# A hybrid RWKV-7 / gated-DeltaNet / SwiGLU layer on one core: the order of high and low products, the width of a small inversion step, the place of the scans' output products, and the planner's estimates

## The chip, the core and the metric

The kernel runs on one core of a Trainium2 chip. The metric is the time of one execution in microseconds (us). Three runs of the kernel before gave 2196.24 us in the median (2191.26 to 2198.05). One execution was recorded by the hardware profiler.

The engines are named as the profile names them: PE does matrix products (PEld is its loading of the stationary operand, which overlaps), DVE is the vector engine, ACT the scalar engine, POOL does a few fills and copies, and SP issues nearly all DMAs.

## What is computed

One layer of a backbone over 256 latent tokens and 256 context tokens, model width 2048. All inputs and outputs are fp32. Cut to what matters:

```python
h  = modulate(rmsnorm(x, norm1_w), sh1, sc1);  hc = the same for ctx
rw, cv, z, ab, gt = split(h @ w_in)              # and of hc @ w_in
# branch a: RWKV-7, 16 heads of 64, forward and backward scans, context before latent
s = s * w_t - (s @ kk_t) b_t + v_t k_t;   y_t = s @ r_t
# branch b: gated DeltaNet, 8 heads of 128, chunks of 64, forward and backward
u, wk = triangular_solve(I + strict(kb k^T * decay), [v * beta, kb * exp(g)])
v_new = u - wk @ s;  o = q_dec @ s + qk @ v_new;  s = s * g_last + k_tail^T @ v_new
m = sigmoid(g_a) * (o_a @ p_a) + sigmoid(g_b) * (o_b @ p_b)
x = x + gt1 * (m @ w_out)
x = x + gt2 * swiglu(modulate(rmsnorm(x, norm2_w), sh2, sc2), w_gate_up, w_down)
return rmsnorm(x, final_norm_w)
```

## The kernel before

**Two-part products.** Every product with a large weight matrix is done with operands split in two: a value is cast to fp32r (the high part, `whi` for weights and `hxh`, `hch` for activations), and what the cast left over is the low part (`wlo`, `hxl`, `hcl`). A product is then high*high + weight-high*activation-low + weight-low*activation-high, three matmuls of 128x128x256 for each 128 rows of depth. For a weight tile ACT casts `whi` from the loaded `wraw`, and after it DVE subtracts to get `wlo`; both work on quarters of four depth blocks (128x512).

**Stages.** (1) Norms, modulation and the first narrow products (0 to about 124 us of the span). (2) One long stage, "the weave" (lines 329 to 1830, from 124.5 to 1337.5 us), with the input projection, both token mixers, and the merge products. (3) The rest of the merge, the output projection and the feed-forward part, in an order written out by hand (1337.5 us to the end at 2188.6).

**The weave and its planner.** Each piece of work of stage 2 is a Python generator that yields operations (`Op`), lists of them, pauses, or things it waits for (a PSUM bank, a named event). `Weave.run` (line 274) is a list scheduler that runs when the program is built: it keeps a clock for each engine, picks the piece whose next operation could start first by its own estimates (`Lane.product`, `Lane.cost` and the table `LAT`), breaks ties by rank, and emits it. What it emits is the order of the instructions on PE, DVE, ACT and POOL; the chip keeps that order and waits on semaphores. So the estimates set an order and never a time. The line number of almost every instruction of the weave is that of the helper which emits it (L164), so groups are told apart by their tiles.

**The pieces that matter here.**
- `products` (line 1255) runs the large products in a stream: `k`, `v`, `r` for eight pairs of RWKV heads, `K`, `V`, `Q` for eight DeltaNet heads, `g` for gates, and later `p`, `b`, `f`, `l` for the merge. For each quarter it waits until the cast of `whi` and `wlo` has been emitted, then for each depth block it issues high*high, high*low and low*high in turn. `cast` (line 1164) fills `whi` and `wlo`, of which there are four quarters each (rings `his`, `los`); both are handed back at the quarter's end.
- `invert` (line 635) inverts unit triangular 64x64 blocks, 16 of two halves for a pair of RWKV heads (`inverse`), 8 for a DeltaNet head (`head_inverse`). Blocks of 16 are inverted on DVE, then merged 16 to 32 and 32 to 64 by small PE products. The 16-to-32 step takes the list `fours` (line 694): one 32x32 stationary part with 16 moving columns for each unit, half and block; a first run of them, two SCALAR_TENSOR_TENSOR on DVE (`Qm`), and a second run. For a pair of heads a run has 64 matmuls, for a DeltaNet head 32.
- `scan` (line 1017) walks the chunks of two pairs of heads at once, in nine calls of four steps. A step has a first group of PE products (`VX` by `LAl` or `LAc`), a copy on ACT to `R1`, products of that with the inverse (`Tx`), then a group with an identity and with the scan's outputs (stationary `VX`, moving `LAl`), copies to `VX` on ACT, and a third group whose sums DVE scales into the next `VX` and adds into the output `Y`. The sums live in PSUM banks `psb` (two): the first is taken at the step's start, the second (`acc`) after the products with the inverse.

Matmuls whose stationary part is smaller than 128x128 use a part of the array; going from one such part size to another, or to the full array and back, is called a turn below.

Of the kernel before, what the change touches and what calls it, by code (L numbers as in the profile page):

```python
# [18 lines left out]
P = 128  # L19
# [11 lines left out]
LAT = dict(dma=3.1, v=1.0, s=1.0, hop=dict(e=0.215, v=0.135, s=0.15, g=0.1), slack=0.1, own=0.09, grp=32, crank=-1, cg=4, into=0.14, back=0.2, cross=0.14, stay=0.0, gpace=1.6)  # L31
# [74 lines left out]
class Op:  # L106


    def __init__(self, lane, cost, call, mode=None, base=None):
        self.lane, self.cost, self.call, self.mode, self.base = lane, cost, call, mode, base  # L110


class Lane:
# [5 lines left out]
    def product(self, out, a):  # L119
# [8 lines left out]
        if rows < 64:  # L128
            return 0.0165, mode
        if rows == 64:  # L130
            return (0.064 if n > 64 else 0.048) if m < P else 0.02 + n * 4 / 2400, mode
        return (0.06 if m < 64 else 0.058), mode
# [17 lines left out]
    def __getattr__(self, name):  # L150

        def op(out, *a, **k):
# [4 lines left out]
            mode = base = None  # L157
            if name == "transpose" and len(a) == 2:
                cost, mode = 0.109, "full"
            elif name == "matmul":  # L160
                cost, mode = self.product(out, a)
            else:
                cost, base = self.cost(name, out, a, k), (out.offset // out.ap[0][0], out.shape[0])
            return Op(self, cost, lambda: getattr(self.engine, name)(out, *a, **k), mode, base)  # L164
# [53 lines left out]
class Weave:  # L218


    def __init__(self):
        self.work, self.free, self.done, self.now, self.mode, self.cur, self.idle = [], {}, {}, 0.0, "full", None, True
# [45 lines left out]
    def release(self, banks):  # L268
        banks.free.append(self.cur.shown())

# [3 lines left out]
    def run(self):  # L274
        while self.work:
# [37 lines left out]
            for o in ops:  # L313
                if lane is self.tensor:
                    cost += self.turn(o.mode)
                    self.mode = o.mode
# [12 lines left out]
def emit(ctx: ExitStack, tc, A, out, dbg=None):  # L329
# [305 lines left out]
    def invert(pool, Lt, parts, nu, which, full, fill, half_way=None, early=None):  # L635
# [53 lines left out]
        def Nt_(h, u):  # L689
# [4 lines left out]
        fours = [(h, u, 32 * b, slice(64 * h + 32 * b, 64 * h + 32 * b + 32)) for u in range(nu) for h in range(2) for b in range(2)]  # L694
        qm = pool.tile([P, 256], F32, tag="qm", name="Qm") if half_way else xt
        Qm = qm[:, :16 * nu].rearrange("p (u c) -> p u c", c=16)
        ps = yield pib
        pv = ps[:, 0:32 * nu].rearrange("p (k u c) -> p k u c", k=2, c=16)
        yield [e.matmul(pv[r, 0, u], Lt(h, u)[b:b + 32, b:b + 32], T0[r, u, b + 16 * (u // h2):b + 16 * (u // h2) + 16],
                        start=True, stop=True) for h, u, b, r in fours]  # L700
        for d in range(2):
            yield v.scalar_tensor_tensor(Qm[:, us[d]], pv[:, 0, us[d]], low16[:, d:d + 1],
                                         eye16[:, d].unsqueeze(1).to_broadcast([P, h2, 16]), ALU.mult, ALU.add)
        yield [e.matmul(pv[r, 1, u], Tx[r, u, b:b + 32], Qm[r, u, :], start=True, stop=True) for h, u, b, r in fours]
        for h in range(2):
            yield [(s.copy if h else v.tensor_copy)(T0[r, us[d], b + 16 * d:b + 16 * d + 16], pv[r, 1, us[d]])
                   for d in range(2) for b in (0, 32) for r in (slice(64 * h + b, 64 * h + b + 32),)]
# [21 lines left out]
        qo = qm[:, 128:256].rearrange("p (i c) -> p i c", c=32) if half_way else pool.tile([P, h2, 32], F32, tag="ivo", name="qo")  # L729
# [75 lines left out]

    def lowrank_out(p, j, ps, so):
# [4 lines left out]
        if j == 3:  # L811
            weave.ready("lowrank", p)
# [204 lines left out]
    def scan(r):  # L1017
# [25 lines left out]
        for m in range(4):  # L1043
# [5 lines left out]
            ops = []  # L1049
            for q, o, n, vx, la, cs_ in todo:  # L1050
                for d, j, h in dh:
                    w = slice(0, P) if n else half[1 - j]
                    ops.append(e.matmul(ps[h, P * q + 64 * d:P * q + 64 * d + 64], la[d][w, cm[d], j, 0:64],
                                        vx[w, 4 * d + cm[d], j, :], start=True, stop=True))
            yield ops
            R1 = rs.tile([P, T], F32, tag="y2", name="R1")
            yield s.copy(R1[:, part], ps[:, part])
            yield [e.matmul(ps[h, T + P * q + 64 * d:T + P * q + 64 * d + 64], o["Tt"](j, 8 * d + cs_[d]),
                            R1[h, P * q + 64 * d:P * q + 64 * d + 64], start=True, stop=True)
                   for q, o, n, vx, la, cs_ in todo for d, j, h in dh]  # L1060

# [8 lines left out]
            for q, o, n, vx, la, cs_ in todo:  # L1070
                if 0 < n < 7:
                    for j, h in enumerate(half):
                        ops.append(add(c3(acc[h, P * q:P * q + P]), j, ident[h, h], vx[h, both, j, :]))
# [4 lines left out]
            if ops:  # L1078
                yield ops
# [66 lines left out]
    gate_next = iter(range(40))  # L1146

    def gate_out(pool, j, ps):
# [4 lines left out]
        if j == 39:  # L1153
# [10 lines left out]
    def cast(parts, i):  # L1164

        for q, part in enumerate(parts):
# [5 lines left out]
            yield s.copy(hi[:, :n], raw[:, :n])  # L1172
            lo = yield los
            yield v.tensor_sub(lo[:, :n], raw[:, :n], hi[:, :n].bitcast(F32))
            raws.put(raw)
            casts[i, q] = hi, lo
            weave.ready("cast", i, q)
# [77 lines left out]
    def products():  # L1255
# [53 lines left out]
        while todo or ahead:  # L1309
# [8 lines left out]
            if what == "l":  # L1318
                yield "cast", i, 0
                hi, lo = casts.pop((i, 0))  # L1320
# [771 lines left out]
```

## Time and profile before

| | |
|---|---|
| median of three runs | 2196.24 us |
| profiled execution, first to last instruction (span) | 2188.6 us |
| median less span | 7.6 us |
| stage 1 / the weave / stage 3 | 124.5 / 1213 / 851 us |
| DVE, ACT busy over the span | 71%, 51% |
| PE instructions in the profile | 24536 matmuls, 24536 weight loads |

The page gives no time of its own for the profiled execution apart from its span. An fp32 matmul shows as two records in the profile, an fp32r matmul as one. The view of groups lists instructions by line, engine and tiles, with the busy time, the mean length and the idle time just before them; the view of waits lists who waited for whom; the timeline lists instructions in order of time; the view of windows gives each engine's busy time and the granted PE clock in a stretch. PE's ends are modelled and overlap the next start, so the distance from start to start is what one matmul costs.

### The profile page before, as it was taken

What the parts mean: (1) busy time and instruction counts of PE and PEld (TensorE: products, weight loads), DVE (VectorE), ACT (ScalarE), POOL (GpSimd) and SP (SyncE); (2) the same over time, 40 slices, a digit from 0 to 9 for tenths busy, and PEclk for the clock granted to TensorE, in tenths of its full rate; (3) what the DMA queues carried; (4) which work ended last, traced back from release to release, by engine and by line L of the source; (5) the groups of instructions that cost most, each with busy time, mean ns of one, the idle gap of its engine ahead of it and who ended that gap; (6) DMA issues with size and microseconds to landing.
All of it is one profiled execution on the core that took longest, in us unless ns stands there. A gap on an engine that the chain in (4) does not pass through costs nothing.

```text
span 2188.6 us, 59116 instructions
## 1 busy us (share of the span) xinstructions
PE 2108.6 (96%) x24536; PEld 1977.7 (90%) x24536; DVE 1552.5 (71%) x3308; ACT 1118.2 (51%) x2209; POOL 19.2 (1%) x55
## 2 busy tenths in 40 slices
PE   7999999999999999999999998999999999999997
PEld 5897698889888888998989987999999999999997
DVE  4466589889889976899998776865666665555554
ACT  3246654565455556565565754644444444444443
POOL 0000000000000000000000000000000000000000
PEclk9999999999999999999999999999999999999999
DMA  9966756645555554665653754856777776666665
GB/s 377 415 175 196 228 154 179 178 144 156 154 167 143 166 164 135 188 194 171 176 152 112 216 153 157 297 177 201 238 248 235 242 241 217 194 191 194 195 194 163
DMA packets 276286, 431.14 MB, mean 197 GB/s; under 512 B 119857, under 2 KB 136625, under 8 KB 271665
## 3 DMA queue, kind: packets, MB, share of 16 engines
q1 hardware_dynamic: 262192, 402.19, 59.5%
q10 hardware_dynamic: 13824, 25.17, 3.6%
q8 instruction: 192, 3.15, 0.6%
q14 instruction: 78, 0.63, 0.1%
HBM read 401.50 MB, written 25.77 MB: 195 GB/s over the span
## 4 chain that ended last, share of the span: by engine, by line
PE 80%; DVE 7%; DMA 7%; ACT 3%; issue 2%; SPq 0%; DVEq 0%; ACTq 0%
PE mm L164 26%; PE mm L438 12%; PE mm L436 12%; PE mm L437 12%; PE s L164 6%; PE pa L164 5%; PE pi L164 3%; DVE arena L164 2%; DMA wraw<-w 2%; DVE wlo L164 2%; DMA wraw<-ada_rest 1%; PE mm L529 1%; PE s L579 1%; ACT arena L164 1%; PE mm L579 1%
## 5 line engine op out<-in xcount | busy, mean ns | idle before, releaser
L427 DVE TENSOR_TENSOR wlo<-wraw,whi 128x1024 fp32r<-128x1024 f32 (+1 forms) x264 | 314.9, 1193 | 291.0 <-ACT whi L426 291.0
L426 ACT CAST whi<-wraw 128x1024 fp32r<-128x1024 f32 (+1 forms) x264 | 270.6, 1025 | 386.1 <-PE mm L437 359.5
L164 PE MATMUL mm<-hxh,wlo 128*128 128x256 f32 x1376 | 399.9, 291 | 9.5 <-DVE wlo L164 7.7
L164 PE MATMUL mm<-hxh,whi 128*128 128x256 f32 x1376 | 397.0, 288 | 2.3 <-ACT whi L164 1.3
L164 PE MATMUL mm<-hxl,whi 128*128 128x256 f32 x1376 | 395.4, 287 | 0.0
L438 PE MATMUL mm<-hfh,wlo 128*128 128x256 f32 x1344 | 371.8, 277 | 0.2 <-DVE wlo L427 0.2
L436 PE MATMUL mm<-hfh,whi 128*128 128x256 f32 x1344 | 371.2, 276 | 0.0
L437 PE MATMUL mm<-hfl,whi 128*128 128x256 f32 x1344 | 371.2, 276 | 0.0
L164 ACT CAST whi<-wraw 128x512 fp32r<-128x512 f32 (+1 forms) x398 | 242.8, 616 | 214.9 <-PE mm L164 93.2
L164 DVE TENSOR_TENSOR wlo<-wraw,whi 128x512 fp32r<-128x512 f32 (+1 forms) x398 | 270.3, 682 | 86.2 <-ACT whi L164 79.8
L164 PEld LDWEIGHTS mm<-hxh,wlo 128*128 128x128 f32 x1376 | 260.7, 189 | 19.6 <-DVE wlo L164 11.3
L164 PEld LDWEIGHTS mm<-hxh,whi 128*128 128x128 f32 x1376 | 260.6, 189 | 10.3 <-issue 4.3
L164 PEld LDWEIGHTS mm<-hxl,whi 128*128 128x128 f32 x1376 | 260.8, 190 | 6.3 <-issue 3.9
L438 PEld LDWEIGHTS mm<-hfh,wlo 128*128 128x128 f32 x1344 | 252.4, 188 | 1.2 <-DVE wlo L427 0.8
L437 PEld LDWEIGHTS mm<-hfl,whi 128*128 128x128 f32 x1344 | 252.5, 188 | 0.0
L436 PEld LDWEIGHTS mm<-hfh,whi 128*128 128x128 f32 x1344 | 252.4, 188 | 0.0
L164 PE MATMUL mm<-hch,wlo 128*128 128x256 f32 x496 | 142.5, 287 | 0.0
L164 PE MATMUL mm<-hcl,whi 128*128 128x256 f32 x496 | 142.2, 287 | 0.0
L436 PE MATMUL mm<-za,whi 128*128 128x256 f32 x512 | 141.5, 276 | 0.0
L164 PE MATMUL mm<-hch,whi 128*128 128x256 f32 x496 | 141.3, 285 | 0.2 <-issue 0.2
L438 PE MATMUL mm<-za,wlo 128*128 128x256 f32 x512 | 141.3, 276 | 0.0
L437 PE MATMUL mm<-za,whi 128*128 128x256 f32 x512 | 141.3, 276 | 0.0
(407 smaller groups left out, 4534.2 us busy)
## 6 DMA issues: line engine op xcount, KB each, us to landing
wraw<-w SPq DMA_DIRECT2D x344, 256.0 KB, 3.3
wraw<-wgu SPq DMA_DIRECT2D x168, 512.0 KB, 4.7
aw<-ada_first SPq DMA_DIRECT2D x32, 1024.0 KB, 12.2
wraw<-wdn SPq DMA_DIRECT2D x64, 448.0 KB, 3.7
wraw<-ada_rest SPq DMA_DIRECT2D x96, 256.0 KB, 3.2
aw<-ada_rest SPq DMA_DIRECT2D x48, 512.0 KB, 4.4
wraw<-wout SPq DMA_DIRECT2D x64, 256.0 KB, 5.7
aw<-ada_gt ACTq DMA_DIRECT2D x64, 256.0 KB, 5.0
```

Of the source, the lines that this page charges most:

```text
L164: return Op(self, cost, lambda: getattr(self.engine, name)(out, *a, **k), mode, base)
L426: S.copy(hi[:, c, :M], raw[:, c, :M])
L427: V.tensor_sub(lo[:, c, :M], raw[:, c, :M], hi[:, c, :M].bitcast(F32))
L436: E.matmul(ps, hi, Xh[:, k, :n], start=first and i == 0, stop=False)
L437: E.matmul(ps, hi, Xl[:, k, :n], start=False, stop=False)
L438: E.matmul(ps, lo, Xh[:, k, :n], start=False, stop=last and i == len(wt) - 1)
L529: E.matmul(ps[32 * g:32 * g + 32, 0:P], ckr[:, k].rearrange("p a b -> p (a b)"), aws[e, c][:, i, g], start=k == 0, stop=k == KT - 1)
L579: E.matmul(ps[:m, T * a:T * a + T], w_, X[:, 2 * e + k, :], start=e == k == i == 0, stop=e == NE - 1 and k == 1 and i == len(todo) - 1)
```

## The change

Four things are changed in the weave; stages 1 and 3 are as before.

**1. High first, low last.** In a quarter all products with `whi` are issued first and those with `wlo` after them. The piece waits for the cast of `whi` at the quarter's start and for that of `wlo` between, and hands each ring back on its own.

Below is PE's order in the merge products `mm<-oa` (the activation's high and low part share the tile `oa_...`, with tile numbers to tell quarters apart). Before:

```order
L164 MATMUL mm_17143<-oa_16582,whi_1610 128x256 x2
L164 MATMUL mm_17143<-oa_16582,wlo_1612 128x256
L164 MATMUL mm_17143<-oa_16582,whi_1611 128x256 x2
L164 MATMUL pa_17165<-arena_1603,CR_81 128x256
L164 MATMUL mm_17143<-oa_16582,wlo_1613 128x256
L164 MATMUL mm_17143<-oa_16582,whi_1611 128x256
```

and of the change:

```order
L170 MATMUL mm_16420<-oa_15756,wlo_1613 128x256 x4
L170 MATMUL mm_16420<-oa_15756,whi_1611 128x256
L170 MATMUL s_16440<-St_16412,arena_1603 128x128 x2
L170 MATMUL mm_16420<-oa_15756,whi_1611 128x256 x7
L170 MATMUL mm_16420<-oa_15756,wlo_1613 128x256 x4
```

The first `wlo` product of a quarter stood behind two products of that quarter; it stands behind eight now (behind sixteen where latent and context tokens go together, as in `k`, `v`, `K`, `V`; behind four there before).

**2. The 16-to-32 step on 64x64 parts.** One matmul with a 64x64 stationary part and 32 moving columns takes the place of two with 32x32 and 16.

PE's order at the first run of this step, in the inversion of the second pair of heads (`pi` is the PSUM bank). Before:

```order
L164 MATMUL mm<-hxh,wlo 128x256
L164 MATMUL mm<-hxh,whi 128x256
L164 MATMUL mm<-hxl,whi 128x256
L164 MATMUL pi<-arena 32x16 x64
L164 MATMUL mm<-hxh,wlo 128x256
L164 MATMUL pa<-C,arena 128x128 x2
```

and of the change:

```order
L170 MATMUL mm<-hxh,wlo 128x256 x2
L170 MATMUL pa<-LAl,arena 64x128 x16
L170 MATMUL mm<-hxh,wlo 128x256 x2
L170 MATMUL mm<-hxh,whi 128x256
L170 MATMUL mm<-hxl,whi 128x256
L170 MATMUL pi<-arena 64x32 x32
```

The run has half as many matmuls. Over the whole program there are 19443 matmuls before and 18675 now, 768 fewer, all of them here: 16 runs that go from 64 to 32 and 16 that go from 32 to 16.

**3. The scans' outputs in the first group.** A step takes both PSUM banks at its start, issues the output products behind `VX` by `LAl`/`LAc`, and issues the identity's products in one list with those by the inverse.

PE's order in one step of a scan. Before:

```order
L164 MATMUL s<-VX,LAl 64x64 x4
L164 MATMUL s<-VX,LAc 64x64 x4
L164 MATMUL mm<-hxh,whi 128x256
L164 MATMUL mm<-hxl,whi 128x256
L164 MATMUL pa<-LAl,arena 64x128 x16
L164 MATMUL s<-R_7194,Tx 64x64 x8
L164 MATMUL s<-VX,C 64x128 x4
L164 MATMUL s<-LAl,VX 64x64 x4
L164 MATMUL mm<-hxh,wlo 128x256
```

and of the change:

```order
L170 MATMUL s<-VX,LAl 64x64 x4
L170 MATMUL s<-VX,LAc 64x64 x4
L170 MATMUL s<-LAl,VX 64x64 x4
L170 MATMUL pa<-C,arena 128x128 x2
L170 MATMUL pa<-wraw,CR 32x256 x2
L170 MATMUL mm<-hxh,wlo 128x256
L170 MATMUL s<-R_6016,Tx 64x64 x8
L170 MATMUL s<-VX,C 64x128 x4
L170 MATMUL pa<-C,wraw 128x64 x2
```

The outputs (`s<-LAl,VX`, 128 stationary rows by 64) moved from behind the 64x64 parts to the group that has their own part size. In the weave's order a turn from one small part size to another occurs 87 times before and 51 times now; visits of small parts from the full array are 230 and 237.

**4. Estimates and order.** `LAT` has other costs of turns, `product` other costs of small parts, a new function `fetched` makes the planner's PE wait for 256-instruction pieces of its program, and `Weave.add` shifts each piece's rank by a drawn number of up to 8 (`NUDGE`). Two events (`lowrank`, `gates`) count their parts instead of naming the last one.

The diff, cut to its core:

```diff
-LAT = dict(dma=3.1, ..., into=0.14, back=0.2, cross=0.14, stay=0.0, gpace=1.6)
+LAT = dict(dma=3.1, ..., into=0.1, back=0.22, cross=0.115, stay=0.0, gpace=1.6, fetch=3.6, land=2.3)
+NUDGE = (46, 8.0)
...
     def add(self, rank, gen, at=None):
         now, cur = self.now, self.cur
+        if cur is None and rank < 800:
+            rank += NUDGE[1] * (2 * self.draw.random() - 1)
...
+    def fetched(self, t, n):
+
+        self.inst += n
+        while self.inst > 256 * self.chunk + 200:
+            self.asked = max(t, self.asked + LAT["fetch"])
+            self.lands.append(self.asked + LAT["land"])
+            self.chunk += 1
+        return max(t, self.lands[(self.inst - 1) // 256])
...
-        fours = [(h, u, 32 * b, slice(...)) for u in range(nu) for h in range(2) for b in range(2)]
+        units = [(h, u, half[h]) for u in range(nu) for h in range(2)]
...
-        yield [e.matmul(pv[r, 1, u], Tx[r, u, b:b + 32], Qm[r, u, :], start=True, stop=True) for h, u, b, r in fours]
+        yield [e.matmul(second[r, 32 * u:32 * u + 32], Tx[r, u], Qm[r, 32 * u:32 * u + 32], start=True, stop=True) for h, u, r in units]
...
             ps = yield psb
+            acc = yield psb
...
+            for q, o, n, vx, la, cs_ in todo:
+                if n >= 4:
+                    for d, j, h in dh:
+                        ops.append(add(acc[h, T + 64 * d:T + 64 * d + 64], j, vx[:, 4 * d + cm[d], j, :], la[d][:, cm[d], j, 64:P]))
             yield ops
...
-            acc = yield psb
...
-            for k in range(nk):
-                if k % CG == 0:
-                    ask(NQ, k == nk - CG)
-                    yield "cast", i, k // CG
-                    hi, lo = casts.pop((i, k // CG))
-                for j, (w, part) in enumerate(((hi, 0), (hi, 1), (lo, 0))):
...
+            for q in range(0, nk, CG):
+                ask(NQ, q == nk - CG)
+                for t, ring, parts in (("h", his, (0, 1)), ("l", los, (0,))):
+                    yield t, i, q // CG
+                    w = casts.pop((t, i, q // CG))
+                    for k in range(q, q + CG):
+                        for part in parts:
...
+                    ring.put(w)
```

More of the change, by code (lines that the diff above doesn't have):

```diff
@@ L29 @@
 GATES_A, GATES_B = ((36,0,0,0,0,0,0,0),(0,0,0,0,0,4,0,0))
-LAT = dict(dma=3.1, v=1.0, s=1.0, hop=dict(e=0.215, v=0.135, s=0.15, g=0.1), slack=0.1, own=0.09, grp=32, crank=-1, cg=4, into=0.14, back=0.2, cross=0.14, stay=0.0, gpace=1.6)
+LAT = dict(dma=3.1, v=1.0, s=1.0, hop=dict(e=0.215, v=0.135, s=0.15, g=0.1), slack=0.1, own=0.09, grp=32, crank=-1, cg=4, into=0.1, back=0.22, cross=0.115, stay=0.0, gpace=1.6, fetch=3.6, land=2.3)
+NUDGE = (46, 8.0)
 LNEXP = "natural_log_exp_and_others"
@@ L315, in run @@
                     cost += self.turn(o.mode)
+                    cost = self.fetched(start + cost, o.insts) - start
                     self.mode = o.mode
@@ L699, in invert, with by @@
-        yield [e.matmul(pv[r, 0, u], Lt(h, u)[b:b + 32, b:b + 32], T0[r, u, b + 16 * (u // h2):b + 16 * (u // h2) + 16],
-                        start=True, stop=True) for h, u, b, r in fours]
+        first, second = ps[:, :32 * nu], ps[:, 512 - 32 * nu:]
+        def by(t, n):
+            return t.rearrange("p (u b c) -> p u b c", u=n, b=2)
+        yield [e.matmul(by(first, nu)[r, u], Lt(h, u), T0[r, u].rearrange("p (b c) -> p b c", b=2)[:, :, 16 * (u // h2):16 * (u // h2) + 16],
+                        start=True, stop=True) for h, u, r in units]
@@ L810, in lowrank_out @@
         yield 2.5
-        if j == 3:
+        out_lows.append(p)
+        if out_lows.count(p) == 4:
             weave.ready("lowrank", p)
@@ L1048, in scan @@
             ps = yield psb
[L1049 to L1060, printed above, removed]
             acc = yield psb
@@ L1070, in scan @@
             for q, o, n, vx, la, cs_ in todo:
-                if 0 < n < 7:
-                    for j, h in enumerate(half):
-                        ops.append(add(c3(acc[h, P * q:P * q + P]), j, ident[h, h], vx[h, both, j, :]))
+                for d, j, h in dh:
+                    w = slice(0, P) if n else half[1 - j]
+                    ops.append(e.matmul(ps[h, P * q + 64 * d:P * q + 64 * d + 64], la[d][w, cm[d], j, 0:64],
+                                        vx[w, 4 * d + cm[d], j, :], start=True, stop=True))
             for q, o, n, vx, la, cs_ in todo:
@@ L1077, in scan @@
                         ops.append(add(acc[h, T + 64 * d:T + 64 * d + 64], j, vx[:, 4 * d + cm[d], j, :], la[d][:, cm[d], j, 64:P]))
-            if ops:
-                yield ops
+            yield ops
+            R1 = rs.tile([P, T], F32, tag="y2", name="R1")
+            yield s.copy(R1[:, part], ps[:, part])
+            ops = [e.matmul(ps[h, T + P * q + 64 * d:T + P * q + 64 * d + 64], o["Tt"](j, 8 * d + cs_[d]),
+                            R1[h, P * q + 64 * d:P * q + 64 * d + 64], start=True, stop=True)
+                   for q, o, n, vx, la, cs_ in todo for d, j, h in dh]
+            for q, o, n, vx, la, cs_ in todo:
+                if 0 < n < 7:
+                    for j, h in enumerate(half):
+                        ops.append(add(c3(acc[h, P * q:P * q + P]), j, ident[h, h], vx[h, both, j, :]))
+            yield ops
             for q, o, n, vx, la, cs_ in todo:
@@ L1175, in cast @@
             raws.put(raw)
-            casts[i, q] = hi, lo
-            weave.ready("cast", i, q)
+            casts["l", i, q] = lo
+            weave.ready("l", i, q)
     def weights(parts, i):
@@ L1318, in products @@
             if what == "l":
-                yield "cast", i, 0
-                hi, lo = casts.pop((i, 0))
+                for t in "hl":
+                    yield t, i, 0
+                hi, lo = (casts.pop((t, i, 0)) for t in "hl")
                 yield "part", NGH - 1
```

81 lines of the change are left out of this document (45 added, 36 removed).

## The prediction

> **What bounds the kernel now.** I read the page first, then the windows by stage, then PE's waits, then the timeline where PE waits.
>
> The page's first row and the windows of the weave, of three stretches in it and of its end (columns: length, then busy time and count of PE, PEld, DVE, ACT, POOL, granted PE clock, DMA share, GB/s):
>
> ```profile
> PE 2108.6 (96%) x24536; PEld 1977.7 (90%) x24536; DVE 1552.5 (71%) x3308; ACT 1118.2 (51%) x2209; POOL 19.2 (1%) x55
> 124.50:1337.50 1213.00, 1167.11 (x15743) 1059.01 (x15744) 994.59 (x2454) 694.18 (x1615) 18.82 (x50) 0.98 0.57 167
> 260.00:420.00 160.00, 156.46 (x2397) 143.97 (x2396) 142.06 (x330) 83.78 (x213) 4.43 (x12) 1.00 0.60 168
> 1240.00:1337.50 97.50, 89.45 (x943) 84.84 (x942) 68.81 (x178) 51.50 (x109) 0.00 (x0) 0.95 0.51 155
> ```
>
> PE bounds the kernel: 96% busy overall, and 1167.1 of 1213.0 us in the weave, the only stage that changes. What an order can win there is the 45.9 us in which PE stands idle, the time lost at a low clock, and turns between part sizes. DVE comes next, with 142.06 of 160 us in one stretch, so it can't give much.
>
> PE's waits over the whole span (engine, tile and line, releaser, total, times, longest):
>
> ```profile
> PE mm L164 <- DVE wlo L164: 7.7, 15, 1.5
> PE pi L164 <- issue: 5.1, 5, 2.1
> ...
> PE mm L164 <- issue: 1.8, 2, 1.6
> ...
> PE s L164 <- ACT VX L164: 1.5, 3, 0.9
> ...
> PE s L164 <- ACT R L164: 1.4, 2, 1.1
> ...
> PE mm L164 <- ACT whi L164: 1.3, 2, 0.8
> ...
> PE s L164 <- DVE VX L164: 0.7, 1, 0.7
> ```
>
> The longest wait of the weave is for `wlo`. No other single cause is near it but "issue", where nothing in the profile holds PE.
>
> **High first, low last.** The group of those products, on PE and on PEld:
>
> ```profile
> L164 PE MATMUL mm<-hxh,wlo 128*128 128x256 f32 x1376 | 399.9, 291 | 9.5 <-DVE wlo L164 7.7 <-issue 1.6
> L164 PEld LDWEIGHTS mm<-hxh,wlo 128*128 128x128 f32 x1376 | 260.7, 189 | 19.6 <-DVE wlo L164 11.3
> ```
>
> PE's idle time undercounts, since a matmul is drawn 0.28 us long while the next starts 0.115 later (the timeline rows at 424.28 and 424.40 below: 0.12); PEld sees 11.3 us. A low product stood two or four slots behind its quarter's first product and now stands eight or sixteen behind, at 0.115 us each some 0.7 or 1.4 us more. The longest wait was 1.5 us and the mean 7.7 / 15 = 0.5, so nearly all of them should go. What is late next is the high cast, whose wait is 1.3 us now and doesn't move. I take **-9 us**, between 7.7 and 11.3; the ends are -11 and 0 (were the wait to pass whole to `whi`).
>
> **Half the instructions in the 16-to-32 step.** An undisturbed run and two disturbed ones in the timeline of PE (start, length, what, count of records, idle before and releaser), and the program's own queue:
>
> ```profile
> 424.28 0.28 PE L164 MATMUL mm<-hxh,whi 128*128 128x256 f32 x1
> 424.40 0.28 PE L164 MATMUL mm<-hxl,whi 128*128 128x256 f32 x1
> 424.60 1.26 PE L164 MATMUL pi<-arena 32*32 32x16 f32 x128
> 425.79 0.39 PE L164 MATMUL mm<-hxh,wlo 128*128 128x256 f32 x1
> ...
> 427.40 0.43 PE L164 MATMUL pi<-arena,Tx 32*32 32x16 f32 x28
> 429.13 1.24 PE L164 MATMUL pi<-arena,Tx 32*32 32x16 f32 x100 [1.30 <-issue]
> ```
>
> ```profile
> 810.76 1.19 PE L164 MATMUL pi<-arena,Tx 32*32 32x16 f32 x121
> 814.03 0.25 PE L164 MATMUL pi<-arena,Tx 32*32 32x16 f32 x7 [2.08 <-issue]
> ```
>
> ```profile
> q8 instruction: 192, 3.15, 0.6%
> ```
>
> A run of 128 records takes 425.79 - 424.60 = 1.19 us. Two of the runs stop in their midst for 1.30 and 2.08 us, with all inputs there. The instruction queue carried 192 packets; PE has 24536 matmuls and as many weight loads, 49072 together, which is 256 for each packet. A run of 128 records with 128 loads is a whole packet's worth in 1.2 us, where plain products use one in 128 x 0.115 = 15 us. So I read these stops as PE outrunning its program. Both views of "issue" add up to 5.1 + 1.8 = 6.9 us. The change halves such a run to half a packet, and the planner now spaces runs by packets. I take **-7 us**; ends 0 and -9 (0.2 us hidden by the drawn length at each of seven stops).
>
> [...]
>
> **What the parts themselves cost.** In place of 1536 matmuls of 32x32 by 16 there are 768 of 64x64 by 32, a shape that the trace lacks. The nearest rows, with the turns around them:
>
> ```profile
> 669.87 0.28 PE L164 MATMUL mm<-hxh,wlo 128*128 128x256 f32 x1
> 670.08 0.68 PE L164 MATMUL s<-R,Tx 64*64 64x64 f32 x16
> 670.59 0.39 PE L164 MATMUL s<-VX,C 64*64 64x128 f32 x4
> 670.91 0.45 PE L164 MATMUL s<-LAl,VX 128*64 128x64 f32 x8
> 671.29 0.39 PE L164 MATMUL mm<-hch,wlo 128*128 128x256 f32 x1
> ```
>
> ```profile
> 464.26 0.45 PE L164 MATMUL s<-VX,LAl 128*64 128x64 f32 x8
> 464.55 0.40 PE L164 MATMUL s<-VX,LAc 128*64 128x64 f32 x8
> ```
>
> Sixteen records of 64x64 by 64 take 670.59 - 670.08 = 0.51 us, 0.032 each; at that price a run of 64 new records is 2.04 us, 0.85 more than 1.19, and the sixteen long and sixteen half-long runs cost 0.85 x 16 + 0.43 x 16 = +20 us. If a record costs what a 32x32 record does, 1.19 / 128 = 0.0093, a run is 0.6 us: 0.6 x 16 + 0.3 x 16 = -14 us. With half the moving columns of the 64-wide row I halve its price: 64 x 0.016 = 1.02 us, and with the turn out the run is near the 1.19 of before. I take **0**, and keep +20 and -14.
>
> The first run's evictions on DVE grow with the wider result:
>
> ```profile
> L164 DVE SCALAR_TENSOR_TENSOR arena<-pi,C x16: 339/346/353, 264.1 to 809.5; 128x128 f32<-128x128 f32 x16
> L164 DVE SCALAR_TENSOR_TENSOR Qm<-pi,C x16: 248/277/289, 925.6 to 1281.0; 128x64 f32<-128x64 f32 x16
> ```
>
> Sixty-four elements more cost 346 - 277 = 69 ns. The first sixteen gain 128 elements (138 ns), the others 64: 3.3 us on DVE. Large products hide it while DVE waits less than PE; uncovered it is +3.3. I take 0.
>
> **The scans.** The order shows 36 turns fewer between small sizes (87 to 51) and seven visits more from the full array. The turn from `s<-VX,C` to `s<-LAl,VX` above: 670.91 - 670.59 = 0.32 us for two matmuls, where four of one size take 464.55 - 464.26 = 0.29. Two 64x128 ones are at most 0.2, so the turn is some 0.13 us: 36 x 0.13 = 4.7. Seven visits cost a turn in (670.08 - 669.87 = 0.21 less a slot, 0.1): +0.7. **-4 us**, ends -5 and 0. No DMA, DVE or ACT instruction is added.
>
> The added wait is for the second bank at the step's start. Behind it on PE stand the first group and the product stream after it. The bank is free when DVE has added the step before into `Y`:
>
> ```profile
> L164 DVE TENSOR_TENSOR Y<-s,Y x16: 282/292/293, 408.5 to 901.8; 128x128 f32<-128x128 f32 x16
> ```
>
> The first group also needs the `VX` that DVE scales just ahead of that, so the wait is at most 0.29 us a step, and the planner puts other products there. Cost 0; without that cover 0.29 x 32 = +9.3.
>
> **Clock.** Windows on three dips (the last column but two is the clock):
>
> ```profile
> 429.70:433.10 3.40, 3.40 (x67) 3.36 (x56) 1.24 (x5) 0.89 (x2) 0.00 (x0) 0.50 0.61 190
> 579.90:586.70 6.80, 6.71 (x162) 6.33 (x165) 5.76 (x12) 2.28 (x6) 0.00 (x0) 0.50 0.34 105
> 815.40:818.80 3.40, 3.40 (x19) 3.40 (x18) 2.67 (x4) 1.65 (x5) 0.00 (x0) 0.50 0.29 82
> ```
>
> The weave's mean is 0.98, so 0.02 x 1213 = 24 us of it is lost. The dips at 429.7 and 815.4 begin right behind the two stops above, that at 579.9 in such a run. At half speed they cost 13.6 / 2 = 6.8 us. I take **-5 us**; ends -12 (half of all) and +7 (as many new ones).
>
> **The new order of the rest.** Costs and drawn ranks reshuffle everything a little. I counted, from the order at the trace's slot lengths, how much PE work lies between a group on the scans' and heads' banks and the PE group whose result it needs through ACT or DVE: under 1 us in 48 of 220 places before, in 32 of 229 now. The scans' waits above (1.5, 1.4, 0.7) with those of the heads are about 10 us; a third is **-3 us**. Ends -10 and +10, since the rest of the 45.9 us can fall or rise as easily.
>
> **Sum.** -9 - 7 - 4 - 5 - 3 = -28 against the profiled span of 2188.6: 2160.6. The median of the runs is 7.6 us above that span, so 2168 us.
>
> **Rivals.**
> - *Program supply isn't the cause.* The stops and their dips stay: 7 + 5 less, 2180; with the 64-wide price as well, 2200 at worst. For it: only two stops were looked at closely. Against: they stop in mid-run with nothing to wait for. [...]
> - *A run costs by its count of records.* Then the parts win 14 us: 2154. For it: records of 16 columns cost only 0.0093 us, less than any other shape. Against: 64 columns cost 0.032. [...]
> - *The idle time falls further.* Forecast terms take 19 of 45.9 us idle. If 35 go, and the clock's 12: 2145.
> - *The drawn order gives it back.* Idle time stays at 45.9 as other waits grow; turns and clock remain: 2187.
> - *Slower: the scans' chain takes over.* The second bank adds 0.29 us to each of 32 steps. Once products run out before the chain, PE's savings turn into waits and the chain's 9.3 us add to the old time: 2206. Against: `R` and `VX` cost PE 3.6 us of waits in all now, so the chain has slack. A chain that sets the end would show in the last stretch, where 97.5 - 89.45 = 8 us are idle.
>
> **How the numbers follow.** The forecast (2156 to 2180) has 0.45; supply not the cause 0.14; by records 0.08; further 0.12; given back 0.13; slower 0.08. A measurement tells 0.3% (6.6 us) from no change: below 2189.6 is faster, above 2202.8 slower. Half of "given back" and a little of the first rival lie within: faster 0.84, same 0.09, slower 0.07. The range leaves out the last case and the far halves of "further" and "given back": 2144 to 2190; it takes in the records' -14 and, with the forecast's other terms, +20.
>
> **What would show it.** Right: `mm <- DVE wlo` under 2 us; `pi <- issue` under 1; runs of 64 records in about 1.2 us; the weave's clock 0.985 or more; its end near 1310 us, and everything behind it as long as before. Wrong: `whi` in `wlo`'s place, new-shape runs of 2 us, the stops still there, or new waits on `s` and `pa` that make up for what went.

## The result, and the profile after

| | before | after |
|---|---|---|
| median | 2194.65 us (4 runs, 2191.26 to 2198.05) | 2207.74 us (4 runs, 2206.28 to 2213.49) |
| profiled execution: span, own time | 2188.6 us | 2205.0 us, 2206.77 us |
| stage 1 / weave / stage 3 | 124.5 / 1213.0 / 851 us | 126.0 / 1225.2 / 853.9 us |

The ratio is 1.0072, 95% interval 1.0051 to 1.0092: the change made the kernel 0.7% slower. Forecast was 2168 us, in a range of 2144 to 2190. An execution's own time lies 1.8 us above its span (2206.77 against 2205.0), so the profiled execution of before took about 2190.4 us and was a quick one. Of the 7.6 us that the prediction added to its sum, 5.8 were that; its base was the median of three runs, and the median of four lies 1.6 us lower. The change by itself was forecast at -28 us and measured at +13 to +16 (by the medians and by the ratio). Between the two profiled executions the difference is 16.4 us, of which 12.2 lie in the weave and 4.2 in stages 1 and 3, which are as before.

The page's first row and the window of the weave, after (columns as in the prediction):

```profile
PE 2122.8 (96%) x23000; PEld 1993.9 (90%) x23000; DVE 1557.1 (71%) x3308; ACT 1128.0 (51%) x2215; POOL 20.8 (1%) x55
125.95:1351.10 1225.15, 1181.61 (x14207) 1075.83 (x14207) 999.09 (x2453) 702.90 (x1619) 20.42 (x50) 0.98 0.56 165
```

The weave lost 12.2 us. PE's idle time in it hardly moved: 1225.15 - 1181.61 = 43.5 us against 45.9, 2.4 less. What grew is PE's *busy* time, 1167.1 to 1181.6 (14.5 more), with 1536 records fewer. So PE does the same work more slowly, and the place to look is what got a new shape.

PE's waits, after:

```profile
PE mm L170 <- ACT whi L170: 7.5, 10, 2.0
...
PE mm L170 <- DVE wlo L170: 3.5, 3, 2.4
...
PE pa L170 <- issue: 2.2, 1, 2.2
PE pi L170 <- DMA extra<-tscr: 2.1, 1, 2.1
```

The wait for `wlo` fell from 7.7 to 3.5 us, and that for `whi` rose from 1.3 to 7.5: together 9.0 before and 11.0 now. `pi <- issue` (5.1 us) is gone; all "issue" fell from 6.9 to 2.2 us.

The groups of the 16-to-32 step, shapes kept apart, before and then after (after the bar: busy time in us, mean ns, idle time ahead and its causes):

```profile
L164 PE MATMUL pi<-arena,Tx 32*32 32x16 f32 x1024 | 11.8, 185 | 5.2 <-issue 4.9 <-DVE arena L164 0.2
L164 PE MATMUL pi<-arena 32*32 32x16 f32 x1024 | 10.8, 180 | 1.8 <-DVE arena L164 1.8
L164 PE MATMUL pi<-iv,LT 32*32 32x16 f32 x320 | 4.6, 186 | 2.4 <-DVE iv L164 2.4
L164 PE MATMUL pi<-Qm,iv 32*32 32x16 f32 x320 | 3.8, 180 | 0.2 <-issue 0.2
L164 PE MATMUL pi<-Qm,extra 32*32 32x16 f32 x192 | 2.5, 190 | 0.9 <-DVE Qm L164 0.8
L164 PE MATMUL pi<-extra,LT 32*32 32x16 f32 x192 | 2.2, 180 | 0.0
```

```profile
L170 PE MATMUL pi<-arena 64*64 64x32 f32 x512 | 16.6, 220 | 0.5 <-DVE arena L170 0.5
L170 PE MATMUL pi<-arena,Tx 64*64 64x32 f32 x512 | 16.4, 220 | 0.2 <-DVE arena L170 0.2
L170 PE MATMUL pi<-Qm,iv 64*64 64x32 f32 x160 | 6.1, 229 | 0.8 <-DVE Qm L170 0.8
L170 PE MATMUL pi<-iv,LT 64*64 64x32 f32 x160 | 6.1, 221 | 2.2 <-DVE iv L170 1.6 <-DMA iv<-tscr 0.6
L170 PE MATMUL pi<-extra,LT 64*64 64x32 f32 x96 | 3.8, 221 | 2.7 <-DMA extra<-tscr 2.1 <-DVE extra L170 0.5
L170 PE MATMUL pi<-Qm,extra 64*64 64x32 f32 x96 | 3.4, 220 | 0.0
```

Half the records take 52.4 us where the old ones took 35.7: **+16.7 us busy**. The idle time ahead of them fell from 10.5 to 6.4, so the step costs 12.6 us more, as much as the weave's whole loss. One run in the timeline of after:

```profile
261.19 0.28 PE L170 MATMUL mm<-hxh,whi 128*128 128x256 f32 x1
261.40 2.06 PE L170 MATMUL pi<-arena 64*64 64x32 f32 x64
263.38 0.38 PE L170 MATMUL mm<-hch,whi 128*128 128x256 f32 x1
```

It takes 263.38 - 261.40 = 1.98 us for 32 matmuls, 0.062 each, against 1.19 us for the old run of 64. That one sum fits the loss doesn't yet show its cause: every other piece was reordered too. The experiments take that apart.

### The profile page after: what moved, and what is told of

Read it like the earlier page. It is cut to its first block, busy times and chain, and to the rows that moved or that the text cites. A ratio compares the mean times of both kernels' runs of the same rounds, so it can differ in the third digit from the quotient of the medians.

```text
span 2205.0 us, 56065 instructions
## 1 busy us (share of the span) xinstructions
PE 2122.8 (96%) x23000; PEld 1993.9 (90%) x23000; DVE 1557.1 (71%) x3308; ACT 1128.0 (51%) x2215; POOL 20.8 (1%) x55
## 4 chain that ended last, share of the span: by engine, by line
PE 80%; DMA 7%; DVE 6%; ACT 4%; issue 2%; SPq 0%; DVEq 0%; ACTq 0%
PE mm L170 27%; PE mm L458 12%; PE mm L456 12%; PE mm L457 12%; PE s L170 6%; PE pa L170 5%; PE pi L170 3%; DMA wraw<-w 2%; DVE arena L170 2%; DVE wlo L170 1%; DMA wraw<-wgu 1%; PE mm L549 1%; ACT whi L170 1%; PE s L599 1%; DMA wraw<-ada_rest 1%
## 5 line engine op out<-in xcount | busy, mean ns | idle before, releaser
L170 PE MATMUL mm<-hxh,whi 128*128 128x256 f32 x1376 | 374.9, 292 | 9.0 <-ACT whi L170 7.3
L170 PE MATMUL mm<-hxl,whi 128*128 128x256 f32 x1376 | 371.9, 290 | 0.0
L170 PE MATMUL mm<-hxh,wlo 128*128 128x256 f32 x1376 | 277.8, 286 | 3.5 <-DVE wlo L170 3.5
L170 PEld LDWEIGHTS mm<-hxh,wlo 128*128 128x128 f32 x1376 | 214.0, 188 | 11.2 <-issue 4.8
L170 DVE TENSOR_TENSOR arena<-arena 128x512 f32<-128x512 f32 (+17 forms) x522 | 121.0, 233 | 14.2 <-ACT arena L170 6.7
```

## The experiments

Two kinds of kernels were made. In one the planner's *order is held*: it plans with the old operations, and what is emitted in their place differs. In the other the planner *plans anew*. Ratios are to the kernel before, run beside it (its medians there were 2188.6 to 2194.3 us). "Idle" is the span less PE's busy time in the one profiled execution (before 80.0 us, after 82.2). "Half clock" is the sum of the periods in the weave whose granted clock is 0.5 in the trace (before 44.4 us, after 37.5). Both are of one execution. The mean granted clock of before's own executions runs from 0.984 to 0.992, and 0.001 of it is 2 x 0.001 x 2190 = 4.4 us at half clock, so a difference of ten us or so in one pair of traces says little; where it matters, the mean clock over all executions is given.

### The parts of the change, order held

**b_parts64**: before's order, the step on 64x64 parts, with the wider DVE step.

```diff
-yield [e.matmul(pv[r, 1, u], Tx[r, u, b:b + 32], Qm[r, u, :], ...) for h, u, b, r in fours]
+yield [whole(e.matmul(...old...), b, second[r64(h), 32 * u:32 * u + 32], Tx[r64(h), u], Qm[...]) for h, u, b, r in fours]
+# whole: the plan keeps two 32x32 operations, the second emits one 64x64 matmul, the first nothing
```

> The kernel before with its order, but the 16-to-32 step on 64x64 parts (each pair of 32x32 matmuls issued as one). Theory 'price of the parts': +18 us for the matmuls, -7 for the stops that go: 2201 to 2209. Rival 'order': the parts cost what they did, 2190 to 2197. If stops are what matters, pi <- issue goes from 5.1 us to under 1.

Measured: 2198.68 us, ratio 1.0025 (1.0009 to 1.0042): +4.4 us by the medians, +5.5 by the ratio. The page's row and the two largest groups of the step:

```profile
PE 2114.7 (96%) x23000; PEld 1985.1 (91%) x23000; DVE 1555.5 (71%) x3308; ACT 1118.4 (51%) x2209; POOL 19.3 (1%) x55
...
L705 PE MATMUL pi<-arena 64*64 64x32 f32 x512 | 17.0, 220 | 1.8 <-DVE arena L164 1.8
L705 PE MATMUL pi<-arena,Tx 64*64 64x32 f32 x512 | 16.4, 220 | 1.0 <-DVE arena L164 1.0
```

The step's price is that of after (52.4 us busy in all six groups), and its stops are gone, 6.9 us in all. Half clock is 23.9 us in this trace, but that execution took 2194.4 us, 4 under the median; over the twelve the mean clock was 0.9883 against 0.9870 before, an estimated 3 us of time by (1 - 0.9870) x 2193 - (1 - 0.9883) x 2198. So by this estimate about 10 of the 17 us came back, which leaves 7 where 4.4 to 5.5 were measured. Both expectations missed: 2201 to 2209 overlooked that return, 2190 to 2197 had no price.

**a_parts32**: after's order, each 64x64 matmul emitted as the two 32x32 ones, DVE at its old width.

> The change with its order of all engines as it stands, but each 64x64 matmul of the 16-to-32 step issued as the two 32x32 ones of before (and its two DVE steps at their old width). Theory 'price of the parts': a 64x64 matmul by 32 columns costs 0.058 us where two by 32x32 cost 0.034, so some 18 us go, less what comes back as stops in mid-run (up to 7): 2190 to 2197. Rival 'order': the step isn't what costs, the drawn order and its waits are: 2204 to 2209.

Measured: 2216.33 us, ratio 1.0107 (1.0084 to 1.0129), slower than after; neither theory gave that. Its waits:

```profile
PE mm L170 <- ACT whi L170: 8.2, 11, 2.0
PE pi L722 <- issue: 5.3, 5, 2.1
PE pa L170 <- issue: 4.2, 2, 2.3
...
PE mm L170 <- issue: 2.8, 2, 1.6
```

The stops are back, 12.8 us of "issue" with a last row of 0.5, and idle is 98.3 us. PE's busy time is 8.9 us below after's, and 16.1 us more idle than undo that. Its mean clock over six executions is 0.984, after's over four 0.987. So in after's order the wider parts seem to save some 8 us, where in before's they cost some. The stops follow the wider parts, with 1536 records fewer, from both sides: at one order all "issue" goes from 6.9 us to none with them, at the other it comes, from 2.2 to 12.8, with the narrow ones.

**b_low_last**: before's order; within a quarter the high products go first and the low ones last.

```diff
-for k in range(nk): ... for j, (w, part) in enumerate(((hi, 0), (hi, 1), (lo, 0))): ...
+for op in [product(hi, part, k, a, X) for k in ks for part in range(2) for a, X in sides] + [product(lo, 0, k, a, X) for k in ks for a, X in sides]:
+    yield op
```

> The kernel before with its order, only the products inside each quarter permuted: high ones first, low ones last (merge products of the last kind left as they were). Theory 'gain of the prediction': waits of mm for wlo fall from 7.7 to under 2 us and nothing takes their place, 2185 to 2190. Rival 'the wait passes to the high cast': mm <- ACT whi rises from 1.3 to 5 us or more, 2192 to 2198.

Measured: 2193.72 us, ratio 1.0003 (0.9986 to 1.002): nothing. Its waits:

```profile
PE mm L164 <- ACT whi L164: 3.0, 5, 0.9
...
PE mm L164 <- DVE wlo L164: 0.9, 3, 0.4
```

`wlo` lost 6.8 us and `whi` gained 1.7, yet PE's waits in the weave sum to 47.2 us against 45.7. The wait for `wlo` did what it was expected to do, and `whi` stayed under the 5 us of the rival; the rest went to many small waits (`pi <- DVE arena` 2.0 to 3.4, `pa <- DVE arena` 0.6 to 2.1, `s <- ACT lo` 2.7 to 4.0).

### The order

**a_seed1** (`NUDGE = (1, 8.0)` for `(46, 8.0)`) and **a_draw0** (`(46, 0.0)`), on the changed kernel:

> The change with another draw of the rank shifts (seed 1 for 46, same size of 8). If the drawn order is worth little: 2204 to 2211. If it is worth as much as the single edits: off by more than 6 us to either side, with the waits of s, pa and mm making the difference.

> The changed kernel with nothing drawn onto the ranks (NUDGE 8.0 to 0.0), everything else left. Theory A (the draw is what took the rest: with the wider step at +4 us and the products' order at 0, some +9 of the +13 are left): about 2197 to 2201. Theory B (the new estimates or the scans' outputs took it, the draw is as good as none): 2203 to 2212. Theory C (any other order is worth +-20 us with no part in it to be named; drawing 1 for 46 has given +23): anything from 2185 to 2230, and then the waits on s, pa and whi differ from after's by some us each in both directions.

**b_draw46** and **b_draw1** (only the draw, on the kernel before), **b_est** (only `LAT`, `product`, `fetched`), **b_scan** (only the scans' outputs):

> The kernel before with only the draw on the ranks (46, 8.0), estimates, step and scans as before; lists count the low-rank and gate outputs, as the change has it. Theory A (the draw took the rest): 2203 to 2208, by waits on s, pa or whi. Theory B (the draw isn't it): 2190 to 2199. Theory C (each order has its own waits): the time lies anywhere within 2185 to 2225, most likely above 2195, because the order before is one whose stops and waits had been got down.

> The kernel before with another draw on the ranks (1, 8.0), nothing else. Theory C (the order before is one that lies low among the orders this planner gives, and any new one costs 10 to 35 us, most of it as periods at half clock): 2200 to 2225, half-clock time over 50 us. Rival (it was the draw 46 and the scans' edit that were bad by themselves): 2188 to 2198.

> The kernel before with only the new estimates (turns 0.1, 0.22 and 0.115, products by shape, instruction fetches). Theory B1 (the new estimates order the work worse): 2203 to 2215, with larger waits on s and pa. Theory A (they do not matter): 2190 to 2199. If the estimates of fetches do what they say, 'PE pi <- issue' and the other stops fall from 6.9 us below 3, with the 32x32 parts still in.

> The kernel before with only the scans' outputs moved into a step's first group. Theory A (they save turns and nothing else): 2189 to 2194, with some 36 cross turns fewer. Theory S (a second bank of psb held through a step makes others wait, or the fuller first group delays the chain): 2200 to 2210, with waits on pa or psb's tiles grown by over 5 us. Theory C (a new order has its own waits): 2185 to 2225.

**a_est58**: the changed kernel with the estimate of the new shape put at 0.058 us, near the 0.062 that a run of after took.

```diff
-return ((0.108 ...) if n > 64 else 0.032 if n < 64 else ...), mode
+return ((0.108 ...) if n > 64 else 0.058 if n < 64 else ...), mode
```

> The changed kernel with one estimate of the planner put right: a 64x64 matmul by 32 columns is planned at 0.058 us, as measured, and not at 0.032 (a run of 32 was planned 0.8 us short, some 12 us over the weave). Theory E (the order lost because the planner believed the wider step to be that much cheaper): 2192 to 2201, with waits on s, pa and whi some 5-10 us less. Theory C (every other order has its own waits, whatever the estimate): anywhere from 2195 to 2230, no better than after's 2207 with even odds.

Every kernel that was planned anew came out slower than before, whatever was edited. So the last three have no edit to speak of: **b_slack** and **a_slack** move one estimate by a nanosecond, **b_tiny** draws ranks that decide ties alone.

```diff
-LAT = dict(..., slack=0.1, ...)
+LAT = dict(..., slack=0.101, ...)
```

> The kernel before with one estimate of the planner changed by a nanosecond (slack 0.1 to 0.101 us): nothing that an edit could be worth, but the order of TensorE's matmuls differs from the 2020th on. Theory C (the order before lies low among those that this planner gives, and whatever makes it plan anew costs 10 us or more): 2198 to 2220. Theory P (an edit's own mechanism made each re-planned kernel slow): 2186 to 2195.

> The kernel before with a draw of 0.01 on the ranks in place of 8.0 (it decides ties alone; the order differs from the 3417th matmul on). Theory C: 2196 to 2220. Theory P: 2186 to 2195.

> The changed kernel with slack 0.101 us, the order differs from the 2759th matmul on. Theory C: 2203 to 2230, above after's in three cases of four, since its draw of 46 also lies low among its orders (waits besides the step's were no more than before's). Theory P: 2203 to 2212.

| kernel | what is new in it | us | ratio (95%) | PE busy | idle | half clock |
|---|---|---|---|---|---|---|
| b_slack | nothing but an order | 2201.87 | 1.0051 (1.0032 to 1.0070) | 2110.0 | 90.6 | 51.2 |
| b_tiny | nothing but an order | 2204.69 | 1.0064 (1.0047 to 1.0082) | 2113.2 | 87.5 | 58.0 |
| b_scan | scans | 2204.40 | 1.0064 (1.0049 to 1.0079) | 2108.3 | 93.3 | 61.4 |
| b_draw46 | draw | 2207.30 | 1.0066 (1.0040 to 1.0093) | 2115.7 | 86.1 | 64.9 |
| b_draw1 | draw | 2217.30 | 1.0133 (1.0115 to 1.0152) | 2117.3 | 100.4 | 37.5 |
| b_est | estimates | 2225.95 | 1.0167 (1.0134 to 1.0199) | 2116.5 | 114.6 | 64.9 |
| a_draw0 | all but the draw | 2203.46 | 1.0064 (1.0039 to 1.0089) | 2124.7 | 86.6 | 47.8 |
| a_est58 | all, one estimate right | 2207.05 | 1.0086 (1.0069 to 1.0104) | 2123.9 | 87.6 | 41.0 |
| a_slack | all, another order | 2211.78 | 1.0086 (1.0066 to 1.0106) | 2127.2 | 79.9 | 44.4 |
| a_seed1 | all, another draw | 2231.17 | 1.0163 (1.0136 to 1.0189) | 2122.1 | 93.3 | 41.0 |

Time and ratio are of all executions, the last three columns of one. That one took 2217.2 us in a_seed1, 2232.9 in b_est and 2213.2 in a_draw0: 14 under, 7 over and 10 over the median.

A nanosecond in one estimate costs 2201.87 - 2190.96 = 11 us, a draw that settles ties 14 us. These two have before's PE and DVE instructions (x24536, x3308), in another order. With the two larger draws that makes four new orders of before's work, 11 to 29 us over it. So the order of before lies low among those tried of its planner, and an edit that makes it plan anew has to be read against such a loss. Against that, the scans, the draw of 46 and all edits together without a draw are worth nothing that can be told. The page's first rows of b_slack and b_tiny show the form that it takes:

```profile
PE 2110.0 (96%) x24536; PEld 1979.5 (90%) x24536; DVE 1553.9 (71%) x3308; ACT 1121.2 (51%) x2211; POOL 20.1 (1%) x55
```

```profile
PE 2113.2 (96%) x24536; PEld 1982.0 (90%) x24536; DVE 1553.6 (71%) x3308; ACT 1122.3 (51%) x2211; POOL 19.9 (1%) x55
```

Idle is up by 10.6 and 7.5 us, busy by 1.4 and 4.6 at the same work, the latter where more of the weave runs at half clock. That lower clock holds over all their executions: the mean is 0.9845 and 0.9828 against 0.9875 of before beside them, an estimated 7 and 11 us by the same sum as for b_parts64, of mean losses of 11 and 14. No single wait makes it: in b_slack `mm <- DVE wlo` is 7.3 us and all "issue" 6.3, near before's 7.7 and 6.9. Three expectations fell here. b_est was to bring the stops under 3 us and all "issue" is 12.6. b_draw1 was to have over 50 us at half clock and has 37.5; most of its loss is idle time. And a_est58, with the new shape no longer planned 0.026 us too cheap, is no faster than after (1.0086 against 1.0072).

### Half clock and waits

In the traces PE's clock is 1.0 or 0.5, and all 24 stretches at either clock in before's record and 22 in after's, but for the last of each, are whole multiples of one period of 3.41 us (in before two of them at 0.5 from 228.31 us, 57 at 1.0 from 235.14, one at 0.5 from 429.70). I added up PE's idle time in every period of the weave in the 19 traces and asked for the clock of the period behind it (periods that were at half clock themselves left out):

```
idle in a period   periods   next at half clock
under 0.6 us          5849      2
0.6 to 1.3 us          340     29
1.3 to 1.7 us          101     45
1.7 to 2.0 us           38     35
over 2.0 us             44     44
```

So a period with over 2 us of idle, in one wait or in several, was followed by half clock every time, and one with under 0.6 us next to never. **b_fill** and **a_fill** test whether filling waits brings time back: matmuls of `ident` by zeros, added onto an open sum, stand ahead of about twenty matmuls that waited 0.9 us or more, for half of their wait (61 of them in b_fill and 73 in a_fill, by the tables in their kernels, a few more than the expectations say).

```diff
+for _ in range(FILL.get(self.k, 0)):
+    first = self.open is None and k["start"]
+    self.engine.matmul((out if self.open is None else self.open)[:, 0:64], self.ident, self.z, start=first, stop=first)
```

> The kernel before, in its own order, with 59 matmuls of ident by zeros (added onto the open product's sums, or into the waiting matmul's own empty bank) put ahead of 20 matmuls that waited 0.9 us or more for DVE, ACT or a bank: TensorE then works in about half of each such wait, the wait itself is as long. Theory K (a period of 3.41 us at half clock comes when TensorE stood for more than some 1.2 us of the period ahead of it: in ten traces none of 3164 periods with under 0.9 us was followed by one, all 24 with over 2.0 us were): the dips at 228, 580, 1034, 1129 and 1320 us go or shorten, time at half clock in the weave falls from 44 to 15-25 us, at 0.66 us lost per us of dip the time is 2173 to 2184. Theory N (the dips do not come from these waits): half-clock time stays at 40-50 us and the time is 2190 to 2197.

> The changed kernel in its own order with 72 such matmuls ahead of the 21 places at which it waited 0.9 us or more. Theory K: its 37.5 us at half clock fall to 12-22 us, the time to 2190 to 2199; what is left over b_fill (some 12-18 us) is then the wider step's slots. Theory N: 2203 to 2212.

Measured: b_fill 2204.07 us, ratio 1.0069 (1.0051 to 1.0086); a_fill 2204.52, ratio 1.0069 (1.0045 to 1.0094), where after had 1.0072. At a filled place the clock did as theory K says. The window of one dip, after and a_fill:

```profile
231.90:235.30 3.40, 3.40 (x6) 1.46 (x6) 0.00 (x0) 1.78 (x4) 0.00 (x0) 0.50 1.03 337
```

```profile
231.90:235.30 3.40, 3.31 (x20) 2.21 (x18) 0.00 (x0) 2.26 (x5) 0.00 (x0) 1.00 1.02 338
```

What the fillers cost is in their own rows of a_fill:

```profile
L125 PE MATMUL mm<-nothing,C 128*128 128x64 f32 x138 | 17.5, 267 | 0.0
L125 PE MATMUL s<-nothing,C 128*128 128x64 f32 x8 | 1.0, 268 | 0.0
```

Half clock fell from 37.5 to 27.3 us, and the records of all PE's other work cover 2116.9 us in place of 2122.8: 5.9 us back, about half of the dips that went. But the fillers are drawn for 18.5 us, for 14.3 of which PE did nothing else, and idle fell by only 10.4 (82.2 to 71.8). So 14.3 - 10.4 - 5.9 = -2.0 us were left, the difference of the two spans. Theory K's mechanism holds at these places. Its times (2190 to 2199, and 2173 to 2184 for b_fill) and its 12 to 22 us at half clock weren't reached, and no run shows its price of 0.66 us per us of dip; what a dip's removal is worth without the fillers' own time stays open. In b_fill half clock fell only from 44.4 to 37.5 us, not to 15 to 25, and it has a second story, in its waits:

```profile
PE pi L127 <- issue: 10.4, 7, 3.3
```

The fillers shifted every later instruction, and all "issue" rose from 6.9 to 12.0 us (this row, 1.2 on `pa` and 0.4 on `mm`). PE's program can be counted by its records in the trace: two matmuls and two weight loads for an fp32 matmul, one of each for an fp32r one or a transpose, one record for a bare wait (in before 24536, 24536 and 204, together 256.6 for each of the 192 packets of the instruction queue q8). By that count these are the matmuls of the weave that started over 0.45 us late at full clock with no wait of their own:

```
             stops  us     place in the count, modulo 256
before           5   7.3   193 to 196
b_low_last       8   9.4   193 to 196
b_draw46        11  13.0   193 to 196
a_parts32        8  10.2   193 to 196
b_fill           8   8.3   193 to 196
b_parts64        0   0.0   -
after            0   0.0   -
```

Of 84 such stops in all 19 traces 75 stand at those four places of 256, each with the last 256 instructions used up in 1.1 to 5.2 us (a plain stretch of 128 products at 0.115 us takes some 15); the other nine are of 0.5 us. That fits the cause that the prediction inferred, that PE waits for its next 256 instructions. It stays an inference, since the fetch itself isn't in the trace.

### Price and stops apart

In before's trace stops of 0.4 to 2.1 us stood in four of the sixteen steps, the price is paid in all. **b_second4** widens only the second run of four steps (`Tx` by `Qm`, 64x64 by 16 columns, no wider DVE step), **b_second8** that of all eight whole steps; order held.

```diff
+if step[0] in (2, 3, 6, 8):   # b_second8: if len(fours) == 64
+    op.call = (lambda: E.matmul(pv[r, 1, u], Tx[r, u], Qm[r, u, :], start=True, stop=True)) if b else (lambda: None)
```

> The kernel before in its own order, with the second half of the 16-to-32 step (Tx by Qm, 64 matmuls of 32x32 by 16) issued as 32 matmuls of 64x64 by 16 in four of its eight whole steps, those at 363, 429, 654 and 812 us, where stops of 0.6, 1.5, 1.2 and 2.2 us stood; no wider DVE step. If a 64x64 matmul costs 0.058 us whatever it moves: each such run 1.95 us in place of 1.19, +3 us, and stops of 5 to 7 us gone, with the two periods at half clock behind them (2 us each): 2183 to 2190. If stops only move to other runs: 2191 to 2197.

> The same in all eight whole steps: +6 us of matmuls, every 'pi <- issue' stop gone but those in first halves. 2184 to 2192 by the sum, 2193 to 2199 if the time lost in wider parts isn't given back as in b_parts64 (+4 with all runs wide).

Measured: 2192.55 us, ratio 1.0010 (0.9988 to 1.0032), and 2194.13, ratio 1.0018 (1.0000 to 1.0036). In b_second4 a run that had been undisturbed stopped, as the second theory said:

```profile
734.57 1.18 PE L167 MATMUL pi<-arena,Tx 32*32 32x16 f32 x118
738.77 0.39 PE L167 MATMUL pi<-arena,Tx 32*32 32x16 f32 x10 [3.02 <-issue]
```

b_second8 gives the price at 16 columns:

```profile
L710 PE MATMUL pi<-arena,Tx 64*64 64x16 f32 x512 | 20.0, 221 | 2.9 <-DVE arena L167 1.5 <-issue 1.4
```

Three of its eight wide runs, at 663, 740 and 818 us, neither stopped nor lay at half clock and take 1.97 to 1.98 us (a fourth, at 264 us, took 2.17). The first takes 665.27 - 663.29 = 1.98 us, 0.062 for each of 32 matmuls:

```profile
663.29 2.04 PE L710 MATMUL pi<-arena,Tx 64*64 64x16 f32 x64 [0.38 <-DVE arena L167]
665.27 0.38 PE L167 MATMUL mm<-hch,wlo 128*128 128x256 f32 x1
```

So 16 columns cost the 0.062 us that 32 do. In both kernels what the wider runs cost and what they save about cancel within the interval, and no kernel of this study beats before.

## Why the prediction was wrong

The sum of -28 us was 19 us of idle time (9 + 7 + 3) and 9 us of busy time (4 + 5) won in the weave. The trace has 2.4 us of idle time won and 14.5 us of busy time lost. So two things failed: the price of the new shape, which was put at nothing, and the taking of each wait that goes as time won.

- **High first, low last (-9): failed at "nearly all of them should go", counted as time.** The low wait fell (7.7 to 3.5, and to 0.9 with the order held), but no time came of it: b_low_last has a ratio of 1.0003, so the term was 0, its stated end. In after `whi` rose to 7.5 us, against "the high cast, whose wait is 1.3 us now and doesn't move". In b_low_last `whi` took only 1.7 of the 6.8 us, and small waits elsewhere took the rest. So that the wait passes to the high cast is one way in which it came back, not the only one; what sets the pace behind them wasn't tried.
- **Instructions in the step (-7): right.** The stops went with the wider parts in both orders (5 to 0 in before's, 8 to 0 in after's), and these all stand at 193 to 196 of 256. The stop of 2.2 us on `pa` in after isn't one of them, since that matmul has a wait of its own. Most packets come without a stop: before's span has 192, its weave 5 stops, of 7.3 us together.
- **The parts' own price (0): a miss of +16.7 us busy.** The step that failed is "with half the moving columns of the 64-wide row I halve its price". The price of a matmul here goes by the part and not by the columns: 0.062 us for 64x64 by 16 and by 32, 0.064 by 64 (two records of 0.032). The end of +20 us had used the 64-column price unhalved and was nearly right; that was the nearest row, and as it stood it would have given 2168 + 20 = 2188 us.
- **DVE's wider step (0): right**, waits for `Qm` are 1.4 us before and 1.3 after.
- **Scans (-4): not seen in the time.** b_scan's PE is as busy as before (2108.3 us) with 17 us more at half clock, where b_tiny with 14 us more is busy 4.6 us longer; so perhaps some 5 us of work went, and idle took it back; two single traces can't show it. The slower rival didn't come: after has no wait of `s` for `Y`, which frees the second bank, and in the weave's last 98.1 us PE stands idle for 7.2, where the prediction had 8 of 97.5.
- **Clock (-5): not seen.** Half clock fell by 6.9 us in the pair of traces, worth an estimated 3.4 us (half of it), which lies within what before's own executions differ by. The mean in the weave stayed at 0.98, and that over after's four executions is 0.987, as before's.
- **The new order (-3, within +-10): failed.** Counting how much work lies between a group and what it needs gave 48 close places before and 32 after, and was no guide: an order with nothing but a nanosecond changed cost 11 us. The rival "the drawn order gives it back" came nearest, with idle time that stays (43.5 us against its 45.9); it had no price for the parts, and so ended at 2187.

What the parts come to in the time depends on the order. The step's +16.7 us of busy time stand in the traces of both orders. With before's order held the wider parts cost 4 to 6 us (b_parts64); with after's order held, taking them out made the kernel slower, not faster (a_parts32, 1.0107 against after's 1.0072, intervals that overlap by a little). High first is worth 0 in before's order (b_low_last). So the parts don't add up to the +13, and some 9 us are not shown apart. A new order is enough to cost that much with no edit at all (b_slack, b_tiny), but those two lose it largely as a lower clock, where after's clock is before's and its loss is busy time. That the scans, estimates and draw of this very kernel add nothing of their own is not shown either, since no kernel could carry them at before's order. What also stays open is why before's order lies 11 us under those next to it.

## What to carry to other kernels

Where a scheduler sets the order, first run a few versions that plan anew with no edit; their gap to the kernel (here 11 to 29 us) is the noise that every planned edit must be read against, and edits are better tried with the order held. Price a new matmul shape by the row with the same stationary part, without scaling by the moving columns (64x64 took 0.062 to 0.064 us here at 16, 32 and 64), and before counting a removed wait as a gain, ask which waits come next: here 6.8 us of one wait went with the order held, and no time. PE's busy time in the weave grew here by 14.5 us with 1536 records fewer, so look at the busy time by shape before looking for new waits.

## What the runs showed of the hardware

- From start to start a 64x64 matmul took 0.062 us by 16 columns (b_second8) and by 32 (after), and 0.064 by 64 (before); one of 32x32 by 16 columns took 0.0186 us (1.19 us for 64, before).
- Of 84 late starts with no wait of their own 75 stand at 193 to 196 of 256 in the count; the longest "issue" of `pi` is 3.3 us (b_fill). The 61 fillers of b_fill, which shift the count, took all "issue" from 6.9 to 12.0 us.
- A period of 3.41 us with over 2.0 us of idle was followed by half clock 44 times in 44, one with under 0.6 us 2 times in 5849. Where fillers took 10.2 us of half clock away in a_fill, the other work of PE got 5.9 us shorter, and the fillers' own time used that up.
